# Sums of the down weights on GpSimd, and x of two quarters loaded and scaled over sixteen ticks

## The chip, the core and the metric

The kernel runs on one core of one Trainium2 chip. The metric is the time of one execution on the device in microseconds; lower is better. TensorE is called PE below, VectorE DVE, ScalarE ACT, GpSimd POOL and SyncE, which here issues all DMAs, SP.

## The reference

One layer of a hybrid decoder in float32, for 2048 tokens of width 1024. Cut to what matters:

```python
hn = rms_norm(h, pre_mix_norm)
proj = hn @ w_in                        # q, k, v, z of 4 delta-rule heads, a and b; f, i, q, g of 4 HGRN2 heads
o_a = gated_delta_rule_chunked(...)     # per head, recurrent over chunks of tokens
o_b = hgrn2_chunked(...)                # per head, recurrent over chunks of tokens
h = h + rms_norm(concat(o_a, o_b) @ w_out, post_mix_norm)
u = rms_norm(h, pre_mlp_norm) @ w_mlp_up
h = h + rms_norm(square(relu(u)) @ w_mlp_down, post_mlp_norm)
h = h + rms_norm(p @ w_ple_proj, ple_norm) * sigmoid(h @ w_ple_gate)
```

The change touches how `w_mlp_down` is prepared and how x reaches the first product. What is computed stays the same.

## The kernel before

**Number format.** Each float32 operand of a large product is split into a rounded part (ACT copies it) and the rest (DVE subtracts), and a product is three matmuls. Line 162 is the copy and line 163 the subtraction of the function `split`.

**Quarters, works, ticks.** The tokens go in four quarters of 512. The stage that the change touches is the input projection with the token mixers, about 45 to 1088 us of the profile. A quarter has 33 works: one for a and b, and eight for each of four head pairs. A work is a product of 24 matmuls of 128x512 (line 1023, `mm`), cut into three ticks of eight matmuls, so a quarter has 99 ticks. Between two ticks the function `tick` runs the steps that stand in an agenda for that tick. A step is a piece of a generator up to its next `yield`, and `at(t, gen, offsets)` enters its steps at ticks t + offset. In this way the delta-rule mixers (`gdn_mixer`), the HGRN2 mixers (`hgrn_mixer`), the preparation of x and the sums of the down weights run beside the products.

**Queues and order.** PE's instructions, and in this stage SP's too, stand in the order in which the program issues them. For DVE, ACT and POOL a scheduler orders the instructions when the kernel is built, from the program's order and from what is ready by its own reckoning. On the chip every engine takes its queue in order: an instruction that waits holds up all behind it.

**The delta-rule mixer's recurrence.** A head has four chunks of 128 tokens, each of three steps a tick apart: PE makes `psa` (line 727) and DVE r_g from it (line 729); PE makes `psb` (line 732) and ACT w_g from it (line 734); PE makes `psc` (line 737) and DVE the new state S_g (line 739), which the next psa reads. Before that DVE solves a triangular system in short rounds of lines 661, 664 and 666 on `sys_g`, which comes by way of two DMAs: ud_g (line 641) and sys_g (line 650). When a head is done, `finish` and `norm_steps` scale its result: the row m_g goes over DVE (line 272), POOL (the power of -0.5, line 158) and the DMAs rd_g (line 276) and rsb_g (line 237) to DVE's scaling og_g (line 556).

**Weights.** In the first quarter the works' weights are loaded and split and the halves kept in DRAM; in the others a work's weights are reloaded on SP, two works ahead (line 183, `w<-cache_in`).

**Sums of the down weights.** The down projection later uses seven products in place of eight (a Strassen-like scheme), and needs sums of the blocks of `w_down`. `down_sums(g)` makes them for g = 0 to 15, in the second to fourth quarter. It takes both buffers of the tag "raw" (512 KB each), loads two blocks into them (line 979, SP), makes four sums in place (lines 982, 983, 985, 986, DVE), and stores both buffers to DRAM (line 990, SP). The batches start at ticks 5, 19, 33, 47, 61 and 75 of the second quarter and at 5, 21, 37, 53 and 69 of the third and fourth; their steps come 0, 4, 6 and 10 ticks after the start.

**x of a quarter.** `load_x(q)` has nine steps: loads of the row of scales and of tiles 0 and 1; loads of tiles 2 to 5 as two pairs into the "raw" buffers (line 959), scaling (line 946) and splitting of tile 0, load of tile 6; scaling and splitting of tile 1, load of tile 7; scaling of tiles 2 and 3, then 4 and 5, then 6 and 7; splitting of the same pairs. Before the change the steps stand at the last nine ticks of the quarter before.

Of the kernel before, what the change touches and what calls it, by code (L numbers as in the profile page):

```python
# [15 lines left out]
ALU = mybir.AluOpType  # L16
# [67 lines left out]
def trunk(ctx, tc, x, xT, pT, vecs, w_in, w_ab, gdn_a_log, gdn_dt_bias, w_out, w_up, w_down,  # L84
          w_ple, w_gate, consts, out):
    nc = tc.nc
    V, S, G, PE = nc.vector, nc.scalar, nc.gpsimd, nc.tensor
# [16 lines left out]
    def blk(c):  # L104
        return slice(c * P, (c + 1) * P)
# [14 lines left out]
    def col(r):  # L120
        return cols[:, r : r + 1]
# [38 lines left out]
    def split(t, eng, raw):  # L160

        S.activation(t[:, 0], raw, AF.Copy)  # L162
        eng.tensor_tensor(t[:, 1], raw, t[:, 0], ALU.subtract)  # L163
# [71 lines left out]
    def spread_load(rd, name, pool=None, tag="rsb", bufs=2):  # L235
        rsb = (pool or st).tile([P, QT], F32, tag=tag, name=f"rsb_{name}", bufs=bufs)
        nc.sync.dma_start(rsb, rd.broadcast_to([P, QT]))
        return rsb
# [8 lines left out]
    def tok(q):  # L247
        return slice(q * QT, (q + 1) * QT)
# [150 lines left out]
    with mixers as mctx:  # L399
# [23 lines left out]
        def x_scale(q):  # L423
            ss2 = sm.tile([P, 2, NC], F32, tag="ss2", name=f"ss2_x{q}")
            rows4 = x[tok(q), :].rearrange("(p c) d -> p c d", c=NC)
            halves, loaded = [(c, a) for c in range(NC) for a in range(2)], []
            for i in range(len(halves) + 1):
                if i < len(halves):
                    c, a = halves[i]
                    t = m2.tile([P, QT], F32, tag="ld", name=f"xs{q}_{c}_{a}", bufs=2)  # L430
                    nc.sync.dma_start(t, rows4[:, c, a * QT : (a + 1) * QT])
                    loaded.append(t)
                if i:
                    c, a = halves[i - 1]
                    t = loaded.pop(0)
                    S.activation(t, t, AF.Square, accum_out=ss2[:, a, c : c + 1])
                yield
            ss = sm.tile([P, NC], F32, tag="ss", name=f"ss_x{q}")
            V.tensor_tensor(ss, ss2[:, 0, :], ss2[:, 1, :], ALU.add)
            V.tensor_scalar(ss, ss, 1.0 / D, EPS, ALU.mult, ALU.add)  # L440
            rsqrt(ss)
            yield
            x_r[q] = spread(ss, f"x{q}")
# [451 lines left out]
        def at(t, gen, offsets):  # L895
            for o in offsets:
                agenda.setdefault(t + o, []).append(gen)

        def call(t, fn):
            def once():  # L900
                fn()
                yield
            at(t, once(), (0,))

        STEPS = SPT = 3
        for q in range(NQ):
            works.append((f"ab{q}", "ab", w_ab, q, None, None, None, None))
            for h in range(4):
                g, b = {}, {}
                t = SPT * len(works)  # L910
# [25 lines left out]
        def load_x(q):  # L936

            rsb = spread_load(x_r[q], f"x{q}", m2, "rsx", 1)
            raws = {}

            def load(k):
                raws[k] = m2.tile([P, QT], F32, tag="ld", name=f"raw_xt{q}_{k}", bufs=2)
                nc.sync.dma_start(raws[k], xT[blk(k), tok(q)])

            def scale(k):
                V.scalar_tensor_tensor(raws[k], raws[k], col(R_PREMIX + k), rsb, ALU.mult, ALU.mult)

            def ready(k):
                t = ra.tile([P, 2, QT], F32R, tag="ring", name=f"xt{q}_{k}")
                split(t, V, raws.pop(k))  # L950
                xts[q].append(t)

            xts[q] = []
            for k in (0, 1):
                load(k)
            yield
            for k in (2, 4):
                t = wp.tile([P, 2, QT], F32, tag="raw", name=f"raw_xt{q}_{k}", bufs=2)
                nc.sync.dma_start(t, xT[k * P : (k + 2) * P, tok(q)].rearrange("(k p) t -> p k t", p=P))
                raws[k], raws[k + 1] = t[:, 0], t[:, 1]  # L960
            for k in (0, 1):
                scale(k)
                ready(k)
                load(k + 6)
                yield
            for k in range(2, KD):
                scale(k)
                if k % 2:
                    yield
            for k in range(2, KD):  # L970
                ready(k)
                if k % 2:
                    yield

        def down_sums(g):

            a = [wp.tile([P, 2, QT], F32, tag="raw", name=f"wd{g}_{i}", bufs=2) for i in range(2)]
            for i in range(2):
                nc.sync.dma_start(a[i].rearrange("p c n -> p (c n)"), w_down[blk(g + i * FF // P // 2), :])
            yield  # L980
            (a11, a21), (a12, a22) = ((t[:, 0], t[:, 1]) for t in a)
            V.tensor_tensor(a22, a22, a21, ALU.add)
            V.tensor_tensor(a21, a11, a21, ALU.subtract)
            yield
            V.tensor_tensor(a11, a22, a11, ALU.subtract)
            V.tensor_tensor(a12, a12, a11, ALU.subtract)
            yield
            for i, names in enumerate((("2", "3"), ("4", "1"))):
                c = dr.tile([P, 2 * QT], F32, name=f"sumd{g}_{i}")
                nc.sync.dma_start(c, a[i].rearrange("p c n -> p (c n)"))  # L990
                for k, n in enumerate(names):
                    sumd[n, g] = c, k

        per_q = SPT * (1 + 8 * 4)
        starts = [per_q * q + 5 + n * i for q, m, n in ((1, 6, 14), (2, 5, 16), (3, 5, 16)) for i in range(m)]
        for g, t in enumerate(starts):
            at(t, down_sums(g), (0, 4, 6, 10))
        for q in range(1, NQ):
            at(per_q * (q - 1) + 30, x_scale(q), range(0, 22, 2))
            at(per_q * q, load_x(q), range(-9, 0))  # L1000
            call(per_q * q, boundary)
        for q in range(2):
            at(0, norm_steps(accs[q], 1.0 / D, EPS, f"e{q}", partial(ple_r.__setitem__, q)),
# [1 line left out]
        with tc.manual_schedule(engines={mybir.EngineType.SP}):  # L1005
# [50 lines left out]
            while clock[0] <= last or len(held) < 2 or 1 in ready:  # L1056
                if fill:
                    q, d = fill.pop(0)
# [602 lines left out]
    for half in range(2):  # L1661
# [4 lines left out]
        for d in range(KD):  # L1666
# [6 lines left out]
            for s, q in enumerate(qs):  # L1673
# [5 lines left out]
                t = es.pop((q, d))  # L1679
# [55 lines left out]
```

## Time and profile before

| | |
|---|---|
| median of 3 runs | 2777.34 us (2775.64 to 2778.69) |
| the profiled execution | 2779.64 us |
| its span, first to last instruction | 2777.8 us |
| busy: PE, DVE, ACT, POOL | 2694.8, 2045.8, 1470.1, 103.8 us |
| mean granted clock of PE | 0.994 |

A row of the busy time by stretch gives for each engine the busy us and in parentheses the number of instructions. A row of a group gives line, engine, operation, `out<-in`, shapes and number, then busy us and mean ns, then the idle time of the engine before it and what ended that. In the timeline a row begins with its start and its length in us; a bracket at its end is the idle time before it and what ended it. PEld is PE's loading of weights, SPq the queue of SP. Tiles bear the program's names without numbers: `wd` are the buffers of the sums, `sumd` their copies in DRAM.

### The profile page before, as it was taken

The numbers are of one execution on the slowest core, as the hardware profiler recorded it, in microseconds if no ns is written. First come the engines' busy times: TensorE is split into PE (matmuls) and PEld (weight loads), VectorE is DVE, ScalarE is ACT, GpSimd is POOL, SyncE is SP. The second block draws the span as 40 slices with busy tenths as digits, with TensorE's granted clock in tenths as the row PEclk, the third lists the DMA queues.
The fourth block names the chain that finished last, engine by engine and source line by source line (L and its number), as shares of the span: only waits on it lengthen the run. The fifth ranks groups of instructions, "written<-read, shape, count | busy, mean of one in ns | idle before, by whom it ended". The sixth has DMA issues, their size and how long they took to land.

```text
span 2777.8 us, 38374 instructions
## 1 busy us (share of the span) xinstructions
PE 2694.8 (97%) x12721; PEld 2216.6 (80%) x12721; DVE 2045.8 (74%) x4242; ACT 1470.1 (53%) x2943; POOL 103.8 (4%) x104
## 2 busy tenths in 40 slices
PE   7999999999999999999899999999999999999999
PEld 5788788788888887777688888887888888887887
DVE  6787877777777677577889767857787765567765
ACT  6665555455546445576555546545455445465421
POOL 0000000000000000000000000001000000001000
PEclk9999999999999999999999999999999999999999
DMA  7777777667666665887466447667454356677663
GB/s 261 261 246 221 238 235 245 218 208 252 216 212 201 213 226 169 274 278 256 139 216 221 170 168 245 220 195 237 160 189 153 139 171 204 194 254 242 216 200 122
DMA packets 268598, 589.24 MB, mean 212 GB/s; under 512 B 55642, under 2 KB 59960, under 8 KB 249200
## 3 DMA queue, kind: packets, MB, share of 16 engines
q1 hardware_dynamic: 268400, 586.79, 63.4%
q8 instruction: 101, 1.65, 0.3%
q14 instruction: 97, 0.79, 0.1%
HBM read 419.75 MB, written 166.92 MB: 211 GB/s over the span
## 4 chain that ended last, share of the span: by engine, by line
PE 58%; DVE 13%; DMA 9%; issue 6%; ACT 3%; SPq 1%; POOL 1%; DVEq 0%; POOLq 0%; ACTq 0%
PE u L1091 22%; PE d L1091 19%; PE mm L1023 7%; PE mmg L1091 6%; DVE pr_g L661 2%; DMA ud_g<-u_g 2%; DVE xs_g L664 1%; DMA sys_g<-ud_g 1%; DVE xs_g L666 1%; PE mmo L1091 1%; DMA rd_g<-m_g 1%; DMA da<-sumd 1%; DMA rsb_g<-rd_g 1%; DMA raw_xt<-in_xT_dram 1%; DMA b<-h1d 1%
## 5 line engine op out<-in xcount | busy, mean ns | idle before, releaser
L1023 PE MATMUL mm<-xt,w 128*128 128x512 f32 x3072 | 775.1, 401 | 2.3 <-DVE acc_vg L505 0.8
L1023 PEld LDWEIGHTS mm<-xt,w 128*128 128x128 f32 x3072 | 560.5, 189 | 113.0 <-DVE acc_vg L505 1.3
L1091 PE MATMUL d<-db,da 128*128 128x512 f32 x2688 | 614.1, 390 | 6.3 <-ACT db L215 4.0
L1091 PE MATMUL u<-t,wu 128*128 128x512 f32 x2604 | 608.1, 396 | 3.3 <-ACT wu L162 3.3
L1091 PEld LDWEIGHTS d<-db,da 128*128 128x128 f32 x2688 | 505.1, 188 | 114.6 <-ACT db L215 5.3
L1091 PEld LDWEIGHTS u<-t,wu 128*128 128x128 f32 x2604 | 489.7, 188 | 121.0 <-ACT wu L162 4.1
L216 DVE TENSOR_TENSOR db<-db 128x512 fp32r<-128x512 f32 x224 | 160.5, 717 | 77.0 <-ACT db L215 75.8
L1420 DVE TENSOR_TENSOR u<-u,u 128x512 f32<-128x512 f32 x224 | 150.3, 682 | 73.2 <-PE u L1091 72.0
L215 ACT ACTIVATE db<-db 128x512 fp32r<-128x512 f32 x224 | 140.8, 629 | 86.1 <-DMA db<-hid 84.1
L1091 PE MATMUL mmo<-mixT,w_out 128*128 128x512 f32 x720 | 172.5, 400 | 8.7 <-DVE w_out L163 6.3
L1091 PE MATMUL mmg<-h2T,wg 128*128 128x512 f32 x768 | 178.2, 394 | 0.0
L1461 ACT ACTIVATE u<-u 128x512 f32<-128x512 f32 x128 | 80.9, 632 | 179.0 <-DVE u L1420 178.6
L1091 PEld LDWEIGHTS mmo<-mixT,w_out 128*128 128x128 f32 x720 | 137.1, 191 | 43.1 <-DVE w_out L163 8.1
L1091 PEld LDWEIGHTS mmg<-h2T,wg 128*128 128x128 f32 x768 | 144.4, 188 | 33.5
L163 DVE TENSOR_TENSOR da<-da 128x512 fp32r<-128x512 f32 x128 | 93.8, 732 | 86.9 <-ACT da L162 86.5
L162 ACT ACTIVATE da<-da 128x512 fp32r<-128x512 f32 x128 | 80.4, 628 | 135.3 <-DMA da<-sumd 100.9
L162 ACT ACTIVATE wu<-a 128x512 fp32r<-128x512 f32 x124 | 74.1, 624 | 49.1 <-DMA a<-in_w_up_dram 47.9
L661 DVE TENSOR_TENSOR pr_g<-xs_g,sys_g 128x16 f32<-128x16 f32 (+14 forms) x240 | 93.8, 391 | 5.3
L226 POOL TENSOR_TENSOR acc_y<-acc_y,sq_y 128x512 f32<-128x512 f32 x28 | 38.2, 1363 | 1398.0 <-ACT sq_y L225 1398.0
L163 DVE TENSOR_TENSOR wu<-a,wu 128x512 fp32r<-128x512 f32 x124 | 84.7, 686 | 4.8 <-ACT wu L162 4.6
L1462 ACT ACTIVATE u<-u 128x512 f32<-128x512 f32 x128 | 80.8, 631 | 3.7
L163 DVE TENSOR_TENSOR da<-dr,da 128x512 fp32r<-128x512 f32 x96 | 66.2, 689 | 16.0 <-ACT da L162 13.6
(374 smaller groups left out, 3802.2 us busy)
## 6 DMA issues: line engine op xcount, KB each, us to landing
w<-cache_in SPq DMA_DIRECT2D x96, 1024.0 KB
db<-hid SPq DMA_DIRECT2D x224, 256.0 KB
cache_in<-w SPq DMA_DIRECT2D x32, 1024.0 KB
hid<-u SPq DMA_DIRECT2D x128, 256.0 KB
da<-sumd SPq DMA_DIRECT2D x128, 256.0 KB
a<-in_w_up_dram SPq DMA_DIRECT2D x124, 256.0 KB
hid<-ht SPq DMA_DIRECT2D x96, 256.0 KB
dr<-in_w_down_dram SPq DMA_DIRECT2D x96, 256.0 KB
```

Source lines behind the costliest of these rows:

```text
L162: S.activation(t[:, 0], raw, AF.Copy)
L163: eng.tensor_tensor(t[:, 1], raw, t[:, 0], ALU.subtract)
L215: S.activation(t[:, 0], plain(t), AF.Copy)
L216: V.tensor_tensor(t[:, 1], plain(t), t[:, 0], ALU.subtract)
L226: eng.tensor_tensor(acc, acc, sq, ALU.add)
L661: V.tensor_tensor(pr[:, :, :, 0:i], xs[:, None, :, 0:i].broadcast_to([P, 2, GC, i]), sys[:, 0:i, i : i + 2].rearrange("p j two -> p two j" ...
L664: V.tensor_reduce(xs[:, :, i : i + 2].rearrange("p g two -> p two g"), pr[:, :, :, 0 : i + 1], AX.X, ALU.add)
L1023: PE.matmul(ps, *terms[i], start=i == 0, stop=i == nt - 1)
L1091: PE.matmul(ps, a, b, start=start, stop=stop)
L1420: V.tensor_tensor(c[new], c[old], ps, ALU.add)
L1461: S.activation(c[k], c[k], AF.Relu)
L1462: S.activation(c[k], c[k], AF.Square)
```

## The change

The four sums of a batch go from DVE (`V`) to GpSimd (`G`), and stand in four steps, at ticks 4, 5, 6 and 7 after the start, in place of two, at 4 and 6. The store stays at 10. The nine steps of `load_x` for the third and fourth quarter stand at 16, 14, 12, 10, 8, 6, 3, 2 and 1 ticks before the quarter's end, those for the second as before. After the first hunk the line numbers grow by two.

```diff
             (a11, a21), (a12, a22) = ((t[:, 0], t[:, 1]) for t in a)
-            V.tensor_tensor(a22, a22, a21, ALU.add)
-            V.tensor_tensor(a21, a11, a21, ALU.subtract)
-            yield
-            V.tensor_tensor(a11, a22, a11, ALU.subtract)
-            V.tensor_tensor(a12, a12, a11, ALU.subtract)
+            G.tensor_tensor(a22, a22, a21, ALU.add)
+            yield
+            G.tensor_tensor(a21, a11, a21, ALU.subtract)
+            yield
+            G.tensor_tensor(a11, a22, a11, ALU.subtract)
+            yield
+            G.tensor_tensor(a12, a12, a11, ALU.subtract)
             yield
...
         for g, t in enumerate(starts):
-            at(t, down_sums(g), (0, 4, 6, 10))
+            at(t, down_sums(g), (0, 4, 5, 6, 7, 10))
         for q in range(1, NQ):
             at(per_q * (q - 1) + 30, x_scale(q), range(0, 22, 2))
-            at(per_q * q, load_x(q), range(-9, 0))
+            at(per_q * q, load_x(q), range(-9, 0) if q == 1 else (-16, -14, -12, -10, -8, -6, -3, -2, -1))
             call(per_q * q, boundary)
```

## The prediction

> **What bounds the kernel now.** I read the page first, then the busy time by stage, then the waits inside the stage that the change touches, and last the timeline around single down-weight sums.
>
> ```profile
> span 2777.8 us, 38374 instructions
> PE 2694.8 (97%) x12721; PEld 2216.6 (80%) x12721; DVE 2045.8 (74%) x4242; ACT 1470.1 (53%) x2943; POOL 103.8 (4%) x104
> ```
>
> The profiled execution took 2779.64 us, of which the span is 2777.8 and 1.8 lies around it; the median of the three runs is 2777.34. My sum is a difference against the profiled execution, and I add it to the median.
>
> All of the change lies in the projection stage of the second to fourth quarter. The busy time by stretch gives the us in which each engine was busy, the granted clock, the DMA share and GB/s:
>
> ```profile
> core 0: us, PE busy (x) PEld busy (x) DVE busy (x) ACT busy (x) POOL busy (x), PEclk, DMA share, GB/s
> 320.00:560.00 240.00, 233.05 (x1271) 196.51 (x1272) 178.91 (x525) 122.18 (x337) 14.72 (x16) 1.00 0.71 235
> 560.00:830.00 270.00, 265.78 (x1448) 224.99 (x1446) 208.47 (x609) 144.16 (x375) 14.90 (x17) 1.00 0.66 221
> 830.00:1088.00 258.00, 253.27 (x1388) 215.55 (x1387) 195.86 (x574) 132.35 (x346) 13.89 (x16) 1.00 0.63 207
> ```
>
> In these 768 us PE is busy 752.1, so 15.9 us is all that better cover could bring. DVE is busy 583.2 us (76%), POOL 43.5 (6%). PE's waits in 320 to 1088, in total, number and longest:
>
> ```profile
> PEld psb_g L732 <- DVE r_g L729: 21.3, 24, 1.8
> PEld psa_g L727 <- DVE S_g L739: 5.4, 9, 1.5
> PE psb_g L732 <- DVE r_g L729: 11.0, 15, 1.3
> ```
>
> These are the recurrence of the delta-rule heads. A head takes four chunks, each of three ticks: psa on PE, r_g on DVE, psb on PE, then psc, and S_g on DVE for the next psa. PE's order is written out, so PE stands whenever DVE has not reached r_g or S_g in its queue. Of the 48 psb (12 heads, four chunks) 24 wait already: a delay of DVE in front of r_g reaches PE about every second time in full. So the question is not how busy DVE is but what stands in its queue at these moments.
>
> **Part 1: the sums move from DVE to POOL.** Removed from DVE are 16 batches of four operations; added to POOL are the same 64, of a shape that POOL runs elsewhere in this kernel (acc_y):
>
> ```profile
> L982 DVE TENSOR_TENSOR wd<-wd,wd x16: 678/682/720, 328.0 to 1019.3; 128x512 f32<-128x512 f32 x16
> L226 POOL TENSOR_TENSOR acc_y<-acc_y,sq_y 128x512 f32<-128x512 f32 x28 | 38.2, 1363 | 1398.0 <-ACT sq_y L225 1398.0
> ```
>
> DVE loses 64 x 0.682 = 43.6 us, POOL gains 64 x 1.363 = 87.2. POOL has room for it. But what does DVE do meanwhile? The timeline of the down projection shows both engines side by side:
>
> ```profile
> 1877.97 1.88 DVE L1524 TENSOR_TENSOR y<-y,d 128x512 f32<-128x512 f32 x3
> 1878.26 1.29 POOL L226 TENSOR_TENSOR acc_y<-acc_y,sq_y 128x512 f32<-128x512 f32 x1 [123.01 <-ACT sq_y L225]
> 1880.30 1.31 POOL L226 TENSOR_TENSOR acc_y<-acc_y,sq_y 128x512 f32<-128x512 f32 x1 [0.74 <-ACT sq_y L225]
> 1880.77 1.38 DVE L216 TENSOR_TENSOR db<-db 128x512 fp32r<-128x512 f32 x1 [0.32 <-ACT db L215]
> 1882.35 1.30 POOL L226 TENSOR_TENSOR acc_y<-acc_y,sq_y 128x512 f32<-128x512 f32 x1 [0.74 <-ACT sq_y L225]
> 1882.83 1.37 DVE L163 TENSOR_TENSOR da<-da 128x512 fp32r<-128x512 f32 x1 [0.67 <-ACT da L162]
> ...
> 1887.00 0.69 DVE L163 TENSOR_TENSOR da<-da 128x512 fp32r<-128x512 f32 x1
> ```
>
> The DVE operation that starts 0.48 us after the POOL operation takes 1.37 instead of 0.69, and ends at 1884.20, which is 0.55 after POOL's end: it was held until 0.14 before that end and then ran in full. The three of L1524, which read one operand from PSUM, run through at 0.63 each. So a POOL operation of this shape holds every DVE operation with two SBUF inputs for up to 1.30 - 0.14 = 1.16 us, more than the 0.68 it saves. L661, L666, L818, L822 and the splits are of that kind; r_g and S_g, with one PSUM input, are not, but they stand behind such ones.
>
> The Trainium skill says the same in SBUF — State Buffer, section "Who interferes with whom": a DVE instruction with two SBUF inputs and a GpSimd instruction that reads SBUF exclude each other for the whole instruction. By that rule the hold would be 1.30 instead of 1.16, and the 9 us taken below would be 10; the trace shows the shorter hold.
>
> "One operation a tick" does not hold on POOL. A tick sets the place in the program, but POOL waits only for the loads and its own results; in the order in which the changed kernel is built the four stand one behind the other in 14 of 16 batches. They start when the load lands, some 6 us after its issue (676.15 - 670.03, the end of the issue, where DVE stood waiting for it):
>
> ```profile
> 669.10 0.93 SPq L979 DMA_DIRECT2D wd<-in_w_down_dram  x2
> 676.15 0.69 DVE L982 TENSOR_TENSOR wd<-wd,wd 128x512 f32<-128x512 f32 x1 [2.23 <-DMA wd<-in_w_down_dram]
> ```
>
> One batch worked through, from the timeline:
>
> ```profile
> 885.93 1.22 SPq L979 DMA_DIRECT2D wd<-in_w_down_dram  x2
> 893.55 0.23 DVE L666 SCALAR_TENSOR_TENSOR xs_g<-xs_g,sys_g 128x4 f32<-128x4 f32 x1
> 893.81 0.52 DVE L661 TENSOR_TENSOR pr_g<-xs_g,sys_g 128x192 f32<-128x192 f32 x1
> 894.76 0.23 DVE L666 SCALAR_TENSOR_TENSOR xs_g<-xs_g,sys_g 128x4 f32<-128x4 f32 x1
> 894.91 0.68 DVE L982 TENSOR_TENSOR wd<-wd,wd 128x512 f32<-128x512 f32 x1
> 895.51 0.34 DVE L729 SCALAR_TENSOR_TENSOR r_g<-vt_g,inv_g,psa_g 128x128 f32<-128x128 f32 x1
> 895.90 0.49 PE L732 MATMUL psb_g<-r_g,xt_full 128*128 128x128 f32 x2 [0.30 <-DVE r_g L729]
> ```
>
> The load lands near 893.3. POOL's first runs to 894.6, L666 is held to 894.5; the second takes over when L666 is done and holds L661 to 895.9 (done 896.4); the third holds the next L666 to 897.6. L982 is gone, so r_g starts near 897.9 instead of 895.5: 2.4 us late, and since psb waited for it already, PE pays them.
>
> How many batches meet such a moment follows from the ticks. Heads do their chunks at ticks 14 to 25 (carried over), 41 to 52, 65 to 76 and 89 to 100 of a quarter of 99; a batch runs from about 2.5 to 5 ticks after its start. Starts 19 and 47 (second quarter) and 69 (third and fourth) lie wholly inside: 4 batches. Start 61 (second), 21 and 37 (third, fourth) lie half inside: 5. The upper bound is 4 x 2.4 + 5 x 1.2 = 15.6 us; the lower is 0, where each held operation has slack. Half of the psb have none and the others some, so I take 9.
>
> The second cost sits in POOL's own queue. In the first batch of each quarter the m_g of a finished head stands behind the four sums:
>
> ```profile
> 585.73 0.90 SPq L979 DMA_DIRECT2D wd<-in_w_down_dram  x2
> 596.24 1.33 POOL L158 TENSOR_TENSOR m_g<-m_g,mhalf 128x4 f32<-128x4 f32 x1 [15.94 <-issue]
> 601.08 0.32 SPq L237 DMA_DIRECT2D rsb_g<-rd_g  x1
> 605.81 0.75 DVE L556 SCALAR_TENSOR_TENSOR og_g<-og_g,cols,rsb_g 128x512 f32<-128x512 f32 x1 [0.75 <-DMA rsb_g<-rd_g]
> 611.23 0.49 PE L732 MATMUL psb_g<-r_g,xt_full 128*128 128x128 f32 x2 [0.92 <-DVE r_g L729]
> ```
>
> The load lands near 592.7, four sums of 1.363 end at 598.2 at best, and with a DVE operation of some 0.5 us between each two at 599.7; m_g was ready at 596.2, so it comes 2 to 3.5 us late (0 if the load lands by 590.8). Its rd_g and rsb_g go through SP, where weight reloads stand behind them (issued two works ahead of their use, so I cost that at 0), and DVE, in order, already stands waiting for rsb_g at L556, with the convolution and r_g behind it, and psb already waits 0.92. I take 2 us three times: 6; bounds 0 and 10.5.
>
> The relief: 43.6 of DVE's 583.2 us is 7.5%, and of the waits of 26.7 us (21.3 + 5.4) that share is 2; I take 3, as the sums stand in single queues in front of r_g (0.30 above). Its bound is all 15.9 of PE's idle time.
>
> **Part 2: x of the third and fourth quarter.** The same 16 scales and splits and 12 DMAs; nothing is removed. The last three steps (the splits of tiles 2 to 7) keep their ticks. The first six move 7 to 2 ticks earlier.
>
> ```profile
> L946 DVE SCALAR_TENSOR_TENSOR raw_xt<-raw_xt,cols,rsb_x x24: 737/744/752, 285.1 to 821.9; 128x512 f32<-128x512 f32 x24
> 453.94 6.57 DMA sumd<-wd
> 803.98 9.71 DMA raw_xt<-in_xT_dram
> 531.28 0.90 SPq L990 DMA_DIRECT2D sumd<-wd  x2
> 534.28 3.13 SPq L641 DMA_DIRECT2D ud_g<-u_g  x4
> 540.95 0.35 DVE L729 SCALAR_TENSOR_TENSOR r_g<-vt_g,inv_g,psa_g 128x128 f32<-128x128 f32 x1 [3.56 <-PE psa_g L727]
> 542.80 0.42 PEld L732 LDWEIGHTS psb_g<-r_g,xt_full 128*128 128x128 f32 x2
> ```
>
> Third quarter: tiles 2 to 5 go into the two buffers of the last batch of sums, and both steps now fall on tick 85. SP issues the stores at 531.3 and must then wait until they have landed (6.57 us in the chain's row), to about 538.3, with the weight reload and ud_g behind it: after three loads and the reload, 0.4 each (L990's row), ud_g goes out at 539.9, 5.6 us late. The x loads land 6.1 (the sums' load above) to 9.71 later, at 544.4 to 548, and in DVE's built order five scales (5 x 0.744 = 3.7 us) stand in front of the r_g of 540.95. It starts at 548 to 551.7, psb was due at 542.8: PE stands 5 to 9 us. The late ud_g falls into that same wait. Six scales, 4.5 us, leave the queue of the later chunks and may give 2 us back. Bounds 0 (loads covered) and 9, taken 7 - 2 = 5. Fourth quarter: the stores are six ticks old, SP does not stop, and the scales fill the 3.56 us in which DVE stood idle before the same r_g; late loads and relieved chunks cancel: 0, bounds -2 and 2.
>
> **Sum.** 9 + 6 - 3 + 5 + 0 = +17 us, all as PE's waits between 320 and 1088: 2777.3 + 17 = 2794. A measurement of this kernel can tell about 0.2%, 5.6 us, from no change.
>
> **Rivals.** *Spread as written*: a batch starts late, or DVE's operations come in between, so that its four operations lie about a tick apart. Then each meets DVE singly: with two of three free ticks the 9 becomes 4, m_g waits for one operation at most (3 x 0.7 = 2), and the sum is 4 + 2 - 3 + 5 = +8: 2785. For it: nothing but the ticks' meaning in the source; against it: POOL's built order and its idle queue.
>
> *DVE's relief decides* (faster): 43.6 us leave the engine that ends PE's waits, the held operations fall into DVE's idle quarter (185 of 768 us), and the x loads land in time. If PE gets back half of its 15.9 idle us, 2769. Of the 64 operations 26 lie in chunk ticks (4 x 4 + 5 x 2); it decides when fewer than one in four of them puts its 1.16 us ahead of r_g, under 7.5 us in all, and m_g is not late. The Trainium skill, Perfetto Trace Analysis, section "Optimizing Scalar/DVE Operations", allows this offloading where DVE is saturated, and warns that the shared read port may undo it. Against it: at 76% DVE isn't full, the solve chain in front of r_g has no idle time, and the holds shown are longer than the savings.
>
> *Off the path*: holds and relief cancel, SP's stop is covered by the idle 3.56 us: -3 to +5, 2774 to 2782.
>
> **How the numbers follow.** Forecast 0.50, spread 0.18, off the path 0.14, relief 0.18. The likeliest case alone reaches from 2784 (each of the three costs half as large: +7) to 2806 (all upper bounds at once would give 15.6 + 10.5 - 3 + 9 = 32, 2809). Taking in the other cases to 2 in 10, 2770 to 2808. Slower by over 0.2%: 0.50 + 0.16 of the second and a little of the third, 0.68; within 0.2%: 0.15; faster: 0.17.
>
> **What would show it.** After: four POOL rows L982 to L988 back to back some 6 us after each L979; L661, L666 and L822 rows of over 1 us beside them; PE's wait on r_g risen above 11.0 us; m_g of POOL 2 to 3 us after its L272; SP waiting after L992 near 532, and a wait of PE of 4 us or more at the psb near 543. I am wrong if the DVE operations beside POOL's keep their lengths, if PE's waits on r_g fall, or if the sums fill the idle stretches of DVE.

## The result, and the profile after

The changed kernel takes 2798.19 us (median of 4 runs, 2796.24 to 2801.3) against 2778.02 for the kernel before: ratio 1.0069, interval 1.0056 to 1.0081, which is +19 us (15.6 to 22.5). The forecast was +17 us.

The engine totals of the page after, and the three stretches of the projection stage. The text counts 320 to 1088 as before, though the work in it has by then slipped by up to 16 us:

```profile
span 2796.3 us, 38389 instructions
PE 2695.9 (96%) x12721; PEld 2215.5 (79%) x12721; DVE 2044.5 (73%) x4178; ACT 1471.4 (53%) x2943; POOL 192.9 (7%) x168
...
320.00:560.00 240.00, 229.18 (x1245) 194.03 (x1246) 175.87 (x490) 121.85 (x334) 47.18 (x40) 0.99 0.71 237
560.00:830.00 270.00, 260.24 (x1420) 219.80 (x1419) 204.16 (x582) 137.78 (x364) 42.70 (x37) 1.00 0.63 216
830.00:1088.00 258.00, 248.29 (x1352) 209.94 (x1350) 186.52 (x527) 130.47 (x342) 42.28 (x36) 1.00 0.62 206
```

DVE has 64 instructions less (4242 to 4178), 43.6 us by their rows. Rows overlap at their edges, so a kernel without any sums (below) has 31.8 us less busy time on DVE (2045.8 to 2014.0). Here it falls by 1.3 us only. GpSimd's rises by 89. PE is busy 737.7 us of the 768, 14.4 less than before; its work is the same, so this is time in which it stands. Its longest waits, PE first, then its weight loads, from 320 to 1108 (us in total, number, longest):

```profile
PE psb_g L732 <- DVE r_g L729: 17.4, 19, 1.7
PE psa_g L727 <- DVE S_g L739: 7.8, 5, 3.0
PE psd_g L685 <- ACT part L713: 2.4, 2, 1.6
PE mm L1025 <- DVE acc_vg L505: 2.0, 3, 0.9
PE kk_g L622 <- ACT y_qg L514: 1.4, 2, 0.7
...
PEld psb_g L732 <- DVE r_g L729: 27.8, 25, 2.2
PEld psa_g L727 <- DVE S_g L739: 11.6, 10, 3.4
```

The same view of before has for PE:

```profile
PE psb_g L732 <- DVE r_g L729: 12.3, 16, 1.3
PE psa_g L727 <- DVE S_g L739: 1.7, 3, 1.1
```

For the weight loads it has 23.0 and 5.4 us there, and it has no wait on ACT at psd_g or kk_g. Three things came: more waiting for r_g, much more for S_g, and a new wait for ACT.

Where did DVE's time go? Into its other operations. The two groups of before that grew most, and the same groups after (busy us, mean ns):

```profile
L666 DVE SCALAR_TENSOR_TENSOR xs_g<-xs_g,sys_g 128x4 f32<-128x4 f32 x256 | 57.6, 225 | 27.6 <-DMA sys_g<-ud_g 22.5
L818 DVE TENSOR_TENSOR qk_h<-qk_h,gg_h 128x256 f32<-128x256 f32 x96 | 39.9, 416 | 8.4 <-ACT keys_h L821 8.3
```

```profile
L666 DVE SCALAR_TENSOR_TENSOR xs_g<-xs_g,sys_g 128x4 f32<-128x4 f32 x256 | 67.0, 262 | 26.0 <-DMA sys_g<-ud_g 20.3
L818 DVE TENSOR_TENSOR qk_h<-qk_h,gg_h 128x256 f32<-128x256 f32 x96 | 45.7, 476 | 9.0 <-ACT keys_h L821 8.9
```

Counted row by row against the median that each operation has in the trace of before, 56 DVE operations beside the 64 sums are longer by over 0.1 us, by 33 us together. The batch that the prediction worked through (wd12), in the timeline after:

```profile
905.96 1.29 POOL L982 TENSOR_TENSOR wd<-wd,wd 128x512 f32<-128x512 f32 x1 [31.10 <-DMA wd<-in_w_down_dram]
906.06 1.22 DVE L666 SCALAR_TENSOR_TENSOR xs_g<-xs_g,sys_g 128x4 f32<-128x4 f32 x1
907.31 0.52 DVE L661 TENSOR_TENSOR pr_g<-xs_g,sys_g 128x192 f32<-128x192 f32 x1
907.33 1.64 POOL L984 TENSOR_TENSOR wd<-wd 128x512 f32<-128x512 f32 x1
907.87 0.36 DVE L664 TENSOR_REDUCE xs_g<-pr_g 128x8 f32<-128x200 f32 x1
908.26 0.73 DVE L666 SCALAR_TENSOR_TENSOR xs_g<-xs_g,sys_g 128x4 f32<-128x4 f32 x1
909.05 1.63 POOL L986 TENSOR_TENSOR wd<-wd,wd 128x512 f32<-128x512 f32 x1
909.46 0.34 DVE L729 SCALAR_TENSOR_TENSOR r_g<-vt_g,inv_g,psa_g 128x128 f32<-128x128 f32 x1
909.85 0.49 PE L732 MATMUL psb_g<-r_g,xt_full 128*128 128x128 f32 x2 [1.75 <-DVE r_g L729]
```

The four sums stand back to back from the landing of the load. L666 took 0.23 before; now it takes 1.22 and 0.73 and ends each time with the sum beside it. L664, with one SBUF input, and r_g, with one operand from PSUM, run at their usual length inside GpSimd's operations. psb waits 1.75 instead of 0.30. And GpSimd waits too: its sums take 1.64 and 1.63 where DVE got in first, 1.29 where GpSimd did.

### The profile page after: what moved, and what is told of

The parts are those of the page before. It is cut to its first block, busy times and chain, and to the rows that moved or that the text cites. A ratio compares the mean times of both kernels' runs of the same rounds, so it can differ in the third digit from the quotient of the medians.

```text
span 2796.3 us, 38389 instructions
## 1 busy us (share of the span) xinstructions
PE 2695.9 (96%) x12721; PEld 2215.5 (79%) x12721; DVE 2044.5 (73%) x4178; ACT 1471.4 (53%) x2943; POOL 192.9 (7%) x168
## 4 chain that ended last, share of the span: by engine, by line
PE 59%; DVE 14%; DMA 9%; issue 4%; ACT 3%; POOL 1%; SPq 1%; DVEq 0%; POOLq 0%; ACTq 0%
PE u L1093 22%; PE d L1093 19%; PE mm L1025 7%; PE mmg L1093 6%; DVE pr_g L661 2%; DMA ud_g<-u_g 2%; DVE xs_g L666 1%; DVE xs_g L664 1%; DMA sys_g<-ud_g 1%; PE mmo L1093 1%; DMA da<-sumd 1%; DMA rsb_g<-rd_g 1%; DMA raw_xt<-in_xT_dram 1%; DMA raw_out<-in_w_out_dram 1%; DMA rd_g<-m_g 0%
## 5 line engine op out<-in xcount | busy, mean ns | idle before, releaser
L661 DVE TENSOR_TENSOR pr_g<-xs_g,sys_g 128x16 f32<-128x16 f32 (+14 forms) x240 | 96.9, 404 | 6.1
L666 DVE SCALAR_TENSOR_TENSOR xs_g<-xs_g,sys_g 128x4 f32<-128x4 f32 x256 | 67.0, 262 | 26.0 <-DMA sys_g<-ud_g 20.3
```

What stands on the lines that cost most here:

```text
L661: V.tensor_tensor(pr[:, :, :, 0:i], xs[:, None, :, 0:i].broadcast_to([P, 2, GC, i]), sys[:, 0:i, i : i + 2].rearrange("p j two -> p two j" ...
L666: V.scalar_tensor_tensor(xs[:, :, i + 1], xs[:, :, i], sys[:, i, i + 1 : i + 2], xs[:, :, i + 1], ALU.mult, ALU.add)
```

## The experiments

Changes in us are the ratio less 1, times the median of before in the same session (2772 to 2774). First the two halves of the change by themselves.

**The sums alone** (e1_sums_only): the change without its last line.

```diff
-            at(per_q * q, load_x(q), range(-9, 0) if q == 1 else (-16, -14, -12, -10, -8, -6, -3, -2, -1))
+            at(per_q * q, load_x(q), range(-9, 0))
```

> The four sums of each of the 16 batches on GpSimd at the new ticks; x loaded and scaled at the old ticks in every quarter. The prediction's terms (9 + 6 - 3): +12 us against before, ratio 1.0043. Rival, from reading when PE reaches the same matmuls before and after: the run after falls behind by some 22 us in all beside GpSimd's sums and at the start of each quarter, and catches up by some 2 near the end of each of the second and third quarter, where x is loaded; then the sums alone cost 18 to 22 us, ratio 1.0065 to 1.008.

Measured: 2787.73 us, ratio 1.0057 (1.0043 to 1.0071): +15.8 us (11.9 to 19.7). PE's wait for S_g is 7.3 us there (1.7 before).

**The spread load alone** (e2_load_only): the kernel before with only the last line of the change.

> The sums stay on DVE with their old ticks; only x of the third and fourth quarter is loaded and scaled over sixteen ticks. The prediction: +5 us (PE stands 5 to 9 us at the psb near 543, less 2), ratio 1.0018. Rival from the traces: PE lost 1.3 us more at that psb and gained more than that in the 40 us behind it, so -1 to -4 us, ratio 0.9986 to 0.9996.

Measured: 2776.39 us, ratio 1.0009 (1.0000 to 1.0017): +2.5 us (0 to 4.7). Together the halves make 18.3 of the 19 us; nearly all is the sums. The rows around the stop of SP in this kernel:

```profile
529.43 0.90 SPq L990 DMA_DIRECT2D sumd<-wd  x2
533.90 1.66 SPq L959 DMA_DIRECT2D raw_xt<-in_xT_dram  x2
536.65 2.69 SPq L641 DMA_DIRECT2D ud_g<-u_g  x4
538.60 1.41 DVE L946 SCALAR_TENSOR_TENSOR raw_xt<-raw_xt,cols,rsb_x 128x512 f32<-128x512 f32 x2 [2.32 <-DMA raw_xt<-in_xT_dram]
541.00 2.08 DVE L946 SCALAR_TENSOR_TENSOR raw_xt<-raw_xt,cols,rsb_x 128x512 f32<-128x512 f32 x3 [0.90 <-DMA raw_xt<-in_xT_dram]
542.99 0.34 DVE L729 SCALAR_TENSOR_TENSOR r_g<-vt_g,inv_g,psa_g 128x128 f32<-128x128 f32 x1
543.39 0.49 PE L732 MATMUL psb_g<-r_g,xt_full 128*128 128x128 f32 x2 [2.07 <-DVE r_g L729]
```

Everything that the prediction named is there: SP stands between L990 and the x loads, ud_g is late, five scales L946 stand in front of r_g, and psb waits. But SP goes on 4.5 us after it issued the stores (533.90), not 7, the loads land 4.7 us after their issue, and PE pays 2.1 us. Over the whole stage (320 to 1108) PE's wait for r_g is 12.2 us here and 12.3 before, so these 2.1 were got back elsewhere. What is new is a wait for ACT of 3.0 us, shown further down.

**No sums at all** (e3_no_sums): the relief of DVE by itself.

```diff
-            V.tensor_tensor(a22, a22, a21, ALU.add)
-            V.tensor_tensor(a21, a11, a21, ALU.subtract)
             yield
-            V.tensor_tensor(a11, a22, a11, ALU.subtract)
-            V.tensor_tensor(a12, a12, a11, ALU.subtract)
             yield
```

> The 64 sums are left out on any engine: the loaded blocks are stored as they are, at the old ticks; x at the old ticks. This is the relief of DVE alone. The prediction: -3 us (7.5% of 26.7 us of waits, and a little), ratio 0.9989. Rival (DVE's relief decides): half or more of PE's 15.9 idle us between 320 and 1088, -8 to -16 us, ratio 0.994 to 0.997.

Measured: 2771.15 us, ratio 0.9989 (0.9979 to 0.9998): -3.1 us (-5.8 to -0.6). To take the sums off DVE, at no cost on any other engine, is worth 3 us. PE's waits for r_g and S_g fall from 14.0 to 11.8 us. This ends the rival that the relief decides: no engine could have taken the sums with more gain than this.

**GpSimd writes and reads nothing** (e8_memset): 64 memsets of the same blocks in the place of the sums.

```diff
-            G.tensor_tensor(a22, a22, a21, ALU.add)
-            ...
+            for t in (a22, a21, a11, a12):
+                G.memset(t, 0.0)
+                yield
```

> In place of each of the 64 sums GpSimd writes zeros into the same 128x512 block: the sums are left out, and GpSimd reads no SBUF for them; ticks, loads and stores as with the sums alone. If the cost is the exclusion of DVE's two-input operations by a GpSimd operation that reads SBUF, DVE's rows keep their lengths and only the relief is left: -3 us, ratio 0.999. If any GpSimd operation of that size holds DVE, or if the cost is GpSimd's queue: +8 to +16 us, ratio 1.003 to 1.006.

Measured: 2770.6 us, ratio 0.9992 (0.9982 to 1.0002): -2.2 us, the relief and no more. The groups of this kernel:

```profile
L983 POOL MEMSET wd<- 128x512 f32 x64 | 31.7, 526 | 213.6 <-DMA wd<-in_w_down_dram 185.4 <-issue 19.2 <-DMA gd<-gb 6.5
L666 DVE SCALAR_TENSOR_TENSOR xs_g<-xs_g,sys_g 128x4 f32<-128x4 f32 x256 | 57.6, 225 | 26.7 <-DMA sys_g<-ud_g 20.9
```

L666 is back at 225 ns. The memsets are shorter than the sums, 0.526 us; but a hold of that length would show on DVE's rows, and the 33 rows of L661, L666, L818 and L822 that run beside a memset keep their lengths of before within 0.02 us. So the price of the sums is not GpSimd's mere activity, but what a GpSimd operation that reads SBUF does to DVE. Nor is it the new order that the scheduler gave DVE: by order of start some 30 of about 1,770 DVE operations stand elsewhere than in the kernel with the sums alone, against some 200 between either of the two and the kernel before. The memsets fill GpSimd's queue for a third of the time only, so they don't settle what the queue costs; the next runs do.

**Where the price falls** (e4_firsts, e5_chunk, e6_outside): the sums of some batches on GpSimd, of the others on DVE, each in two pairs at the old ticks.

```diff
+            E = G if g in (0, 6, 11) else V                          # e4_firsts
+            E = G if g in (1, 3, 4, 7, 8, 10, 12, 13, 15) else V     # e5_chunk
+            E = G if g in (2, 5, 9, 14) else V                       # e6_outside
-            V.tensor_tensor(a22, a22, a21, ALU.add)
+            E.tensor_tensor(a22, a22, a21, ALU.add)
             ...
```

> Only the first batch of each quarter (wd0, wd6, wd11) is summed on GpSimd, in two pairs at the old ticks; the other 13 batches on DVE; x at the old ticks. The prediction: the m_g that stands behind these sums costs 2 us three times, less 3/16 of the relief of 3: +5.4 us, ratio 1.0019; PE then waits longer near 335, 605 and 870. Rival (the lateness of m_g is covered, the cost lies in the chunk ticks): -1 to +1 us, ratio 0.9996 to 1.0004.

> GpSimd sums the nine batches whose four operations fall, wholly or half, into chunk ticks (wd1, 3, 4, 7, 8, 10, 12, 13, 15), in two pairs; the other seven stay on DVE; x at the old ticks. The prediction: 9 less 9/16 of 3, +7.3 us, ratio 1.0026. Rival, from the sums alone (+15.7 measured) and the first batches (0 measured): the hold is the whole of it and falls on these nine, +13 to +18 us, ratio 1.0047 to 1.0065. If the cost is instead a matter of each of the 64 operations, wherever it stands: 9/16 of 15.7, +8.8.

> GpSimd sums only the four batches whose operations fall between the chunk phases (wd2, 5, 9, 14), in two pairs; the other twelve stay on DVE; x at the old ticks. The prediction: no cost, less 4/16 of 3: -0.8 us, ratio 0.9997. The hold confined to chunk ticks says the same, -1 to +1. If each operation costs alike: 4/16 of 15.7, +3.9 us, ratio 1.0014.

Measured: the three first batches 2773.57 us, ratio 1.0000 (0.9991 to 1.0008), 0 us; the nine of the chunk ticks 2781.84 us, ratio 1.0036 (1.0023 to 1.0049), +10.0 us (6.4 to 13.6); the four between the chunk phases 2769.93 us, ratio 0.9994 (0.9982 to 1.0006), -1.7 us (-5.0 to 1.7). The price falls where a recurrence is running: PE's waits for r_g and S_g are 16.8 and 5.7 us in the run of the nine (12.3 and 1.7 before). GpSimd's queue isn't it, for DVE waits 12.0 us for a result of GpSimd (L606 for rk_g) there, as before. In the run of the four outside, L818 grows too (from 416 to 457 ns in the mean), and it costs nothing: PE waits 12.1 us for r_g and not at all for S_g. The first batches show why a late m_g costs nothing:

```profile
597.02 0.15 DVE L272 TENSOR_SCALAR m_g<-m_g 128x4 f32<-128x4 f32 x1
597.16 1.82 POOL L987 TENSOR_TENSOR wd<-wd,wd 128x512 f32<-128x512 f32 x1
598.94 1.20 POOL L158 TENSOR_TENSOR m_g<-m_g,mhalf 128x4 f32<-128x4 f32 x1
600.17 0.32 SPq L276 DMA_DIRECT2D rd_g<-m_g  x1
601.57 0.32 SPq L237 DMA_DIRECT2D rsb_g<-rd_g  x1
606.67 0.75 DVE L556 SCALAR_TENSOR_TENSOR og_g<-og_g,cols,rsb_g 128x512 f32<-128x512 f32 x1
```

m_g starts 1.9 us after its L272 (0.3 before). But rsb_g, which SP issued 3.5 us behind rd_g before (597.59, 601.08), follows here after 1.4. In both traces SP waits for the landing of rd_g there (2.6 and 0.5 us by the waits of its queue). The chain has the two transfers, before and in this run:

```profile
597.59 3.47 DMA rd_g<-m_g
600.17 1.39 DMA rd_g<-m_g
```

It is the same in the other two first batches (3.58 to 2.08 us, and 2.72 to 1.38). So og_g starts 9.65 to 10.03 us behind its L272 in the three batches, and 9.61 to 10.29 before. Why the transfer lands sooner when it is issued later the traces don't settle.

**All sums in pairs** (e9_pairs): the sums alone, but in pairs at the old ticks (0, 4, 6, 10).

> All 16 batches on GpSimd, the sums in pairs at the old ticks (4 and 6 behind the start) instead of one a tick; x at the old ticks. In the order in which it is built GpSimd's queue is the same as with one a tick. If only the hold matters, this costs what the sums alone cost, +15.7 us, ratio 1.0057. If one operation a tick brings a cost of its own, this costs the sum of the three groups measured apart (0 + 10.0 - 1.7), +8 us, ratio 1.003.

Measured: 2784.43 us, ratio 1.0044 (1.0032 to 1.0056): +12.2 us (8.9 to 15.5). It agrees with the sums one a tick within the intervals, and so "one operation a tick" is not seen to do anything. The three groups together make 8.3 us, and the half widths of their intervals combine to some 5; so this run is in reach of the sum of the parts and the first one (15.8) just out of it. Whether the batches cost more together than apart is left open.

**Sums apart in time** (e7_spaced, e10_gaps). First by loads in three steps:

```diff
+            for part in (((0, 1), (1, 1)), ((0, 0),), ((1, 0),)):
+                for i, c in part:
+                    nc.sync.dma_start(a[i][:, c], w_down[blk(g + i * FF // P // 2), c * QT : (c + 1) * QT])
+                yield
```

> All 16 batches on GpSimd as in the run with the sums alone, but the operands are loaded in three steps a tick apart (a21 and a22; then a11; then a12), so that the first sum, the next two and the last start about a tick apart instead of back to back; x at the old ticks. Four loads of half the size take the place of two. The prediction's first rival (4 + 2 - 3): +3 us, ratio 1.001. If the holds add up by their number, however they are spaced: +16 us as with the sums alone, ratio 1.0057.

Measured: 2791.05 us, ratio 1.0067 (1.0052 to 1.0082), +18.6 us. The experiment missed its aim: the loads still landed together, and the sums of wd12, for one, start at 902.28, 903.94, 905.65 and 907.44, back to back as ever. It says nothing on spacing. So the gap was made on GpSimd itself, in the nine batches of the chunk ticks:

```diff
+            def gap(*ts):
+                for t in ts if E is G else ():
+                    G.tensor_tensor(a_gap, t[:, :NC], mhalf, ALU.pow)
             E.tensor_tensor(a22, a22, a21, ALU.add)
+            gap(a22, a21)
             E.tensor_tensor(a21, a11, a21, ALU.subtract)
+            gap(a21, a11)
             ...
```

> The nine batches of the chunk ticks on GpSimd as in the run of these nine, but between two sums GpSimd does two powers of 128x4 (about 1 us each by the row of L158, beside which DVE's rows keep their lengths), whose results nobody uses, so that the sums start about 3.4 us apart. The prediction's first rival, that operations met singly cost less (4 of 9): +4.4 us where back to back cost +10.0, ratio 1.0016. If the holds add up by their number: +10, ratio 1.0036, and as many held rows of DVE as there (32).

Measured: 2788.64 us, ratio 1.0062 (1.0048 to 1.0076): +17.2 us (13.3 to 21.1), worse than back to back (+10.0). GpSimd's row and one held operation:

```profile
904.85 1.64 POOL L991 TENSOR_TENSOR wd<-wd 128x512 f32<-128x512 f32 x1
906.57 2.73 POOL L987 TENSOR_TENSOR a_gap<-wd,mhalf 128x4 f32<-128x4 f32 x2
909.38 1.29 POOL L994 TENSOR_TENSOR wd<-wd,wd 128x512 f32<-128x512 f32 x1
...
909.49 1.46 DVE L822 TENSOR_TENSOR qk_h<-qk_h,gg_h 128x256 f32<-128x256 f32 x1
```

The sums of this batch start 3.7 to 4.5 us apart, 31 DVE rows are held (32 in the run of the nine without gaps), but for 24 us instead of 18.5: 0.78 each instead of 0.58. Spacing spares no hold. Though a batch now takes some 14 us, DVE waits no longer for results of GpSimd (12.0 us at L606 in both runs). PE's waits for r_g and S_g are 25.3 us against 22.5; what makes up the rest of the 7 us is open.

**The spread load without its stop** (e11_load_later, e12_load_no_stop): other ticks for x, sums on DVE.

```diff
-(-16, -14, -12, -10, -8, -6, -3, -2, -1)
+(-16, -13, -11, -9, -7, -6, -3, -2, -1)      # e11_load_later
+(-13, -12, -11, -10, -8, -6, -3, -2, -1)     # e12_load_no_stop
```

> Sums on DVE; x of the third and fourth quarter on the ticks -16, -13, -11, -9, -7, -6, -3, -2, -1. SP's queue still has the x loads into the raw buffers right behind the stores of the sums, so SP stops as before; but in the order built, ACT keeps y_qg ahead of the table load and of e_g at the start of the quarter, as in the kernel before. If ACT's new order is what took back the gain of the spread load: the +2.4 us near 600 and the +1.6 us near 865 are gone, so -1 to -3 us, ratio 0.999 to 0.9996. If SP's stop is what costs (the prediction, +5): as the spread load alone, +2.5 us or more, ratio 1.0009.

> Sums on DVE; x of the third and fourth quarter on the ticks -13, -12, -11, -10, -8, -6, -3, -2, -1. The loads into the raw buffers now stand behind ud_g in SP's queue, and ACT keeps the order of before. The prediction's terms without SP's stop: 0 to -2 us, ratio 0.9993 to 1. From the traces (a gain of 3.8 us behind psb near 543 and of 1 near 846, no loss at the quarters' start): -2 to -5 us, ratio 0.998 to 0.9993. If SP's stop cost nothing in the end, this equals the run with the stop and ACT's old order.

Measured: 2774.36 us, ratio 1.0006 (0.9997 to 1.0016), +1.7 us; and 2773.6 us, ratio 1.0004 (0.9995 to 1.0012), +1.1 us. The expectations were wrong in their premise: in both traces ACT has the new order (y_qg at 603.05 and at 601.01, behind cd_g and part), so they do not take it away. What they do show: without the stop PE's wait for r_g is 8.8 us in total (12.3 before), psb near 541 waits 0.34, and the time is still not below before. What came instead is at the start of the quarter, here in the kernel after the change:

```profile
602.17 0.21 ACT L578 ACTIVATE cd_g<-gf_g 128x4 f32<-128x4 f32 x1 [3.22 <-DMA gf_g<-gd]
605.48 0.55 ACT L713 ACTIVATE part<-psp_g 64x128 f32<-64x128 f32 x2
606.08 0.71 PE L685 MATMUL psd_g<-xt_g,part 128*128 128x128 f32 x4 [1.62 <-ACT part L713]
608.06 1.28 ACT L514 ACT_TABLE_LOAD   x1
609.35 0.63 ACT L514 ACTIVATE y_qg<-acc_qg 128x512 f32<-128x512 f32 x1
610.03 0.49 PE L622 MATMUL kk_g<-y_qg,y_kg 128*128 128x128 f32 x2 [0.72 <-ACT y_qg L514]
```

Before, ACT did y_qg and part first and cd_g behind them:

```profile
596.06 0.63 ACT L514 ACTIVATE y_qg<-acc_qg 128x512 f32<-128x512 f32 x1 [1.91 <-DVE acc_qg L506]
596.71 0.56 ACT L713 ACTIVATE part<-psp_g 64x128 f32<-64x128 f32 x2
599.35 0.21 ACT L578 ACTIVATE cd_g<-gf_g 128x4 f32<-128x4 f32 x1
```

Now cd_g comes first, waits 3.22 us for gf_g, and part, a load of ACT's function table and y_qg stand behind it. That load isn't one more: before it came later, ahead of y_vg (608.22), and both kernels have 68 in all. PE stands at psd_g and kk_g. These two waits, 3.0 to 3.8 us together, are in the four profiles with x moved and in no other; the kernel with loads in three steps has ACT's new order too, but PE doesn't stand there, so the order alone isn't enough. That these waits took back the gain is read from the traces, not shown by a run of its own: a version without the stop and with ACT's old order was not run.

No kernel that makes all the sums is measurably faster than the one before.

## Why the prediction came out

The total was close (+17 against +19), but by luck: two terms that were too large, m_g by 6 us and the load by 2.5, cancel what the holds lacked.

*Holds in the chunk phases, 9 (0 to 15.6).* The mechanism stands: GpSimd operations that read SBUF hold DVE's (the run with memsets), in front of r_g and S_g, in the nine batches that the ticks pointed to. For these nine the prediction's terms give 7.3; measured 10.0 (6.4 to 13.6). The single hold was over-sized: psb of wd12 pays 1.45 more, not 2.4, because L661 got in ahead of GpSimd's second sum and ran at its usual 0.52, where the prediction held it. And S_g was left out of the price: the prediction names its wait, but worked out a delay of r_g alone. In the kernel after PE's wait at psa rose by 6.1 us, more than at psb (5.1).

*m_g behind the first batches, 6 (0 to 10.5).* This step failed. m_g was late as worked out (602.89 after its L272 at 599.67, 3.2 us, in the kernel after), but the three batches by themselves cost 0 (-2.5 to 2.2). The prediction carried 2 us of the lateness through rd_g and rsb_g to L556 and on to PE. In the run of the three rd_g landed 1.3 to 2.1 us sooner after its issue than before, and og_g started within 0.4 us of its old distance from L272. This is not all of the kernel after: there, with x moved as well, og_g comes 1.2 and 1.8 us later behind its L272 in the third and the fourth quarter, and no run tells what PE pays for that.

*Relief, -3.* Measured -3.1 (-5.8 to -0.6), and -2.2 with memsets. The size is right; the share was taken of the waits of the weight loads (26.7 us), where the matmuls themselves waited 12.7 (11.0 and 1.7).

*Load of x, +5 (0 to 9).* Measured +2.5 (0 to 4.7). The stop, the late ud_g and the five scales came as named, but each wait was taken too long: the stores' landing by one row of 6.57 us where SP went on after 4.5, the x loads by 6.1 to 9.71 where 4.7 were needed, so PE stood 2.1 at psb and not 5 to 9, and got these back elsewhere (12.2 us for r_g in all, 12.3 before). That nothing else changes its order was assumed, and is wrong: ACT's order at the start of the third and the fourth quarter changed, and PE stands there for 3.8 us in the kernel after (2.4 and 1.4 above).

*Sum.* All sums cost 12 to 16 us where the terms gave 9 + 6 - 3 = 12: what the m_g term put in too much makes up for what the holds, alone or together, lacked. Of the rivals, "spread as written" fell twice: the sums do stand back to back, and standing apart they cost more. "Relief decides" is bounded by 3 us. "Off the path" holds for 7 of the 16 batches, in the two groups that were run apart.

## What to carry to other kernels

Work moved from DVE to GpSimd was paid here by DVE's two-input operations, even tiny ones on a serial chain: look at what DVE does beside each moved operation, and not at the sum of busy time. Seven batches could be moved for nothing, in groups of three and four, and the nine not, and the gain to be had was 3 us in any case. Bound that gain first, by a kernel that leaves the work out. A late result need not be a cost: follow it to the engine that needs it, and measure how late it is there. And a change of when a step is issued can reorder a third engine (here ACT, whose table load came to stand ahead of y_qg): compare the order on every engine.

## What the runs showed of the hardware

The hold isn't confined to DVE operations with two tensors from SBUF. A TENSOR_SCALAR of 128x4 (usually 0.16) stood for a whole sum in the kernel after:

```profile
865.69 1.35 POOL L986 TENSOR_TENSOR wd<-wd,wd 128x512 f32<-128x512 f32 x1
865.81 1.25 DVE L272 TENSOR_SCALAR m_g<-m_g 128x4 f32<-128x4 f32 x1
```

The Trainium skill, SBUF — State Buffer, section "Who interferes with whom", says so: tensor_scalar can use the shared ports as well, and a GpSimd instruction that only writes does not contend with a second SBUF input. Both agree with this row and with the run of memsets. In that run a TENSOR_SCALAR of 128x16 (L486, usually 0.15) took 0.56 us beside a memset, while the two-input operations weren't held: that a GpSimd operation must read in order to hold DVE is seen for two-input operations only.

By the same section of the Trainium skill whoever comes first gets the ports and the other blocks. Here it goes both ways: the 64 sums take 1.27 to 1.83 us each, by whether DVE got in before them.
